# A hybrid attention layer on one core: x given in both layouts, V of all heads made from unnormalised blocks

## The chip, the core and the metric

The kernel runs on one core of a Trainium2 chip. The metric is device time in microseconds (us), the median of three runs. The engines are named as in the profile: PE is TensorE (matmuls; PEld is its weight load), DVE is VectorE, ACT is ScalarE, POOL is GpSimd, and SP's queue issues the DMAs. "Split" below means that a value is kept as two tiles, hi (a copy by ACT, rounded to the matmul's type) and lo (the rest, by DVE), and that a product is then three matmuls: hi by hi, lo by hi, hi by lo.

## What is computed

One layer on x (1024 tokens, D = 1024, float32), followed by a last RMSNorm. What the change touches is the first line and the projections that read it:

```python
h = rmsnorm(x, g_mix)                     # x * rsqrt(mean(x*x, axis=-1) + 1e-6) * g_mix
proj = h @ w_in                           # 1024 x 2560
q, k, v, p, gb, gc, hin = split(proj)     # 512, 512, 512, 256, 256, 256, 256 columns
att  = diff_attention(q1, q2, k1, k2, v)  # 4 heads, causal, two softmaxes, v of 128 columns each
pool = multiscale_pool(p); conv = gb * causal_conv3(gc * hin)
x = x + concat(att, pool, conv) @ w_o
x = x + swiglu(rmsnorm(x, g_ffn)); out = rmsnorm(x, g_final)
```

## The kernel before

**Layout.** PE contracts over partitions, so the projections need h with D on the partitions: h[c] (c is the half of 512 tokens) is a pair of tiles hi and lo of 128 x 8 x 512, element [p, k, t] being feature k*128 + p of token t. x lies in memory with tokens as rows.

**The first stage** (lines 215 to 239) goes token block by token block, 128 at a time. `load` brings x's block (512 KB), `normed` (L129) squares and sums it on ACT (L118), forms the mean on DVE (L103) and the power -1/2 on POOL (L110), and scales with g_mix on DVE (L135). `turn_split` (L139) turns the eight 128 x 128 pieces on PE (L144) into PSUM, and ACT (L145) and DVE (L146) evict them into hi and lo. Between two blocks' transposes stand the 24 matmuls of 128 x 256 (L199) that make V of heads 0 and 1 for an earlier block (`project_v`, L188). V of heads 2 and 3 is made later, as one of the fill items below. Fourteen matmuls on the identity (L93) open PE's queue, ahead of any data.

**The fill.** The other projections are items of `chain` (L390): 128 columns of w_in each, 48 matmuls of 128 x 512 (L248) in 16 steps, the next item's weights split in the middle of the one before. Items are K and Q of head 0 and pool columns 1, which are put ahead of attention (`n_before = 3 * 16`, L410), then K and Q of the other heads, conv and pool columns, and V of heads 2 and 3. Attention's 25 early blocks (head, 128 queries) are worked off in `scores` (L484), `flip`, `attend` and `put`; `pace` (L675) draws the fill's steps between their parts, so that PE has products while DVE and ACT do the softmax. A scheduler then sets the order of each engine's instructions within these dependencies; every engine works its queue in order.

**The bias table.** Lines 430 to 446 make the table of relative biases that every score block adds: a small matmul (L437), an addition on DVE (L439), and three DMAs one after the other (L441, L443, L445), the last into the tile near, which DVE reads at L503.

**Buffers.** 35 slots of 128 x 1024 float32 hold everything passing; PSUM has two buffers each of a (two banks), c and f (one bank).

## Time and profile before

| | |
|---|---|
| median of three runs | 1084.64 us (1084.09 to 1084.82) |
| the profiled execution | 1085.24 us |
| its span, first to last instruction | 1083.3 us |
| PE busy | 1061.3 us (98%) |
| PEld busy | 891.2 us (82%) |
| DVE busy | 745.1 us (69%) |
| ACT busy | 428.1 us (40%) |
| mean granted clock of PE | 0.997 |

A busy share is an average over stages. What a stage's work is worth is read from the chain of waits (what released each step) and from the table of busy time by stage. Matmuls are pipelined: the duration of one is its latency, and the pace is read from a row of them in the chain.

### The profile page before, as it was taken

What the parts mean: (1) busy time and instruction counts of PE and PEld (TensorE: products, weight loads), DVE (VectorE), ACT (ScalarE), POOL (GpSimd) and SP (SyncE); (2) the same over time, 40 slices, a digit from 0 to 9 for tenths busy, and PEclk for the clock granted to TensorE, in tenths of its full rate; (3) what the DMA queues carried; (4) which work ended last, traced back from release to release, by engine and by line L of the source; (5) the groups of instructions that cost most, each with busy time, mean ns of one, the idle gap of its engine ahead of it and who ended that gap; (6) DMA issues with size and microseconds to landing.
All of it is one profiled execution on the core that took longest, in us unless ns stands there. A gap on an engine that the chain in (4) does not pass through costs nothing.

```text
span 1083.3 us, 13855 instructions
## 1 busy us (share of the span) xinstructions
PE 1061.3 (98%) x5215; PEld 891.2 (82%) x5215; DVE 745.1 (69%) x1321; ACT 428.1 (40%) x764; POOL 61.4 (6%) x89
## 2 busy tenths in 40 slices
PE   7999999999999999899999999999999999999997
PEld 7987888997887887778888888888888888888886
DVE  6549668768687646987777776867776757555554
ACT  6325535546463334532232323323232344343442
POOL 1101001001000002200000000000000000000010
PEclk9999999999999999999999999999999999999999
DMA  7310121102251422235535444543544996476553
GB/s 261 98 31 20 40 78 40 40 2 77 88 175 49 147 98 67 87 117 175 185 108 177 174 144 157 194 157 115 175 171 146 315 361 219 138 225 202 177 203 125
DMA packets 96130, 150.60 MB, mean 139 GB/s; under 512 B 7320, under 2 KB 48832, under 8 KB 96064
## 3 DMA queue, kind: packets, MB, share of 16 engines
q1 hardware_dynamic: 96064, 149.72, 41.2%
q8 instruction: 41, 0.67, 0.3%
q14 instruction: 25, 0.20, 0.1%
HBM read 107.49 MB, written 43.00 MB: 139 GB/s over the span
## 4 chain that ended last, share of the span: by engine, by line
PE 84%; DVE 9%; DMA 3%; ACT 2%; issue 1%; POOL 0%; POOLq 0%; SPq 0%; DVEq 0%; ACTq 0%
PE ps_f L904 17%; PE ps_a L904 11%; PE ps_f L248 10%; PE ps_c L904 10%; PE ps_a L1013 9%; PE ps_f L615 6%; PE ps_c L1013 5%; PE ps_f L1013 5%; PE ps_f L199 4%; PE ps_c L539 2%; PE ps_c L526 1%; PE ps_a L496 1%; PE ps_a L495 1%; PE ps_f L261 1%; DVE k_low L291 1%
## 5 line engine op out<-in xcount | busy, mean ns | idle before, releaser
L51 DVE TENSOR_TENSOR lo<-raw,hi 128x1024 fp32r<-128x1024 f32 (+1 forms) x84 | 93.3, 1134 | 78.1 <-ACT hi L50 72.1
L248 PE MATMUL ps_f<-h,w_hi 128*128 128x512 f32 x448 | 140.8, 395 | 0.6 <-ACT pt L384 0.6
L50 ACT CAST hi<-raw 128x1024 fp32r<-128x1024 f32 (+1 forms) x84 | 81.6, 980 | 119.9 <-DMA raw<-in_w_down 28.2
L904 PE MATMUL ps_c<-b,w 128*128 128x512 f32 x528 | 124.4, 390 | 0.0
L904 PEld LDWEIGHTS ps_c<-b,w 128*128 128x128 f32 x528 | 98.8, 188 | 20.3
L248 PEld LDWEIGHTS ps_f<-h,w_hi 128*128 128x128 f32 x448 | 81.6, 188 | 16.6 <-ACT pt L384 0.9
L110 POOL TENSOR_TENSOR rstd<-ms,nhalf 128x1 f32<-128x1 f32 x56 | 35.1, 627 | 935.1 <-DVE ms L103 873.3
L248 PE MATMUL ps_f<-h,w_lo 128*128 128x512 f32 x224 | 87.6, 391 | 0.5 <-DVE w_lo L170 0.5
L51 DVE TENSOR_TENSOR w<-raw,w 128x512 fp32r<-128x512 f32 x66 | 47.5, 720 | 46.0 <-ACT w L50 46.0
L615 PE MATMUL ps_f<-wo_hi,mix 128*128 128x512 f32 x224 | 75.5, 401 | 0.7 <-ACT mix L50 0.7
L50 ACT CAST w_hi<-s 128x1024 fp32r<-128x1024 f32 x44 | 46.0, 1052 | 61.5 <-DVE s L769 54.2
L50 ACT CAST w<-raw 128x512 fp32r<-128x512 f32 x66 | 41.1, 622 | 59.6 <-PE ps_f L904 27.4
L904 PE MATMUL ps_f<-T,w 128*128 128x512 f32 x264 | 63.7, 390 | 0.0
L508 ACT ACTIVATE e<-ps_a,nm 128x128 f32<-128x128 f32 (+7 forms) x64 | 47.2, 744 | 36.5 <-DVE nm L506 29.3
L51 DVE TENSOR_TENSOR w_lo<-s,w_hi 128x1024 fp32r<-128x1024 f32 x44 | 53.6, 1222 | 10.9 <-DMA kept2S<-sum 2.5
L904 PEld LDWEIGHTS ps_f<-T,w 128*128 128x128 f32 x264 | 49.4, 188 | 10.9 <-DVE low L917 0.6
L1013 PE MATMUL ps_a<-lo,hi 128*128 128x512 f32 (+1 forms) x154 | 57.6, 374 | 0.0
L1013 PE MATMUL ps_a<-hi,lo 128*128 128x512 f32 (+1 forms) x154 | 57.6, 374 | 0.0
L1013 PE MATMUL ps_a<-hi 128*128 128x512 f32 (+1 forms) x154 | 57.5, 374 | 0.0
L904 PE MATMUL ps_f<-t,w_hi 128*128 128x512 f32 x176 | 54.5, 389 | 0.0
L904 PE MATMUL ps_f<-b,w_hi 128*128 128x512 f32 x176 | 54.3, 389 | 0.0
L904 PE MATMUL ps_a<-t,w_hi 128*128 128x512 f32 x176 | 54.2, 389 | 0.0
(204 smaller groups left out, 2318.5 us busy)
## 6 DMA issues: line engine op xcount, KB each, us to landing
raw<-in_w_down SPq DMA_DIRECT2D x37, 512.0 KB, 4.5
raw<-in_w_gate SPq DMA_DIRECT2D x22, 512.0 KB, 5.6
raw<-in_w_up SPq DMA_DIRECT2D x22, 512.0 KB, 4.2
raw<-in_w_in SPq DMA_DIRECT2D x20, 512.0 KB, 3.7
raw<-in_x SPq DMA_DIRECT2D x16, 512.0 KB, 4.6
raw<-in_w_o SPq DMA_DIRECT2D x8, 512.0 KB, 4.3
x<-raw SPq DMA_DIRECT2D x8, 512.0 KB, 2.6
x<-x SPq DMA_DIRECT2D x8, 512.0 KB, 7.5
```

What stands on the lines that cost most here:

```text
L50: nc.scalar.copy(hi, src)
L51: lo_eng.tensor_sub(lo, src, hi.bitcast(F32))
L110: nc.gpsimd.tensor_tensor(r, ms, nhalf, op=ALU.pow)
L199: nc.tensor.matmul(ps[:, tt, :], h[t // 4][b][:, k, cols], ws[k // 4][a][:, k % 4, :], start=k == 0 and j == 0, stop=k == KT - 1 and j == 2)
L248: nc.tensor.matmul(ps, w[a][:, k, :], h[c][b][:, k, :], start=k == 0 and j == 0, stop=k == KT - 1 and j == 2)
L261: nc.tensor.matmul(ps, w[a][:, k, :], h[c][b][:, k, :], start=k == 0 and j == 0, stop=k == KT - 1 and j == 2)
L291: nc.vector.tensor_sub(low[own, s, :], ps[own], t[own, s, :].bitcast(F32))
L508: nc.scalar.activation(es[:, :n], ps[:, :n], AF.Exp, bias=nm, scale=1.0, accum_out=z[:, s:s + 1])
L539: nc.tensor.matmul(av[:, :(2 - a) * DV], pts[j // 4][:, a, (j % 4) * P:(j % 4 + 1) * P], rhs, start=j == 0 and a == 0, stop=j == i and a == 1)
L615: nc.tensor.matmul(wo_ps[t][nh], halves[m, t // 4][:, a, cols], wo[m][b][:, nh * 512:(nh + 1) * 512], start=m == SET_A[0] and j == 0, stop ...
L904: nc.tensor.matmul(ps, w[a][:, k, :], h[b][k], start=new and k == 0 and j == 0, stop=k == 3 and j == 2, skip_group_check=not new)
L1013: nc.tensor.matmul(ps, a_op[a][:, j, i * P:(i + 1) * P], b_op[b][:, j, cols], start=start and p == 0, stop=stop and p == 2, skip_group_che ...
```

## The change

The host gives x a second time as x_t, with tokens as columns, so that blocks arrive with D on the partitions and nothing has to be turned. RMSNorm's factor of a token is then a factor of a column of h and of a row of v:

- Blocks of x_t (256 features by 512 tokens) and of V's 512 columns of w_in are loaded in turn. `gained` makes hi and lo of x times g_mix, g_mix being a scalar per partition (the tile gm, loaded as 1024 single elements). `v_products` multiplies this unnormalised h with V's columns of all four heads, 512 wide, as each pair of blocks lands.
- ACT squares the blocks; `square_sum` adds the squares of the eight features of a partition on DVE; `token_rstd` sums over the partitions with matmuls against two columns of ones, and forms the factor of each token, r, as a column of 128 x 4. `v_out` evicts V with r as a scalar. `along` replicates r, turns it with four transposes and copies it into rbc, so that it lies along the tokens.
- K and Q of head 0 for half 0 come from the unnormalised h too, and are multiplied with rbc at eviction (`of_gained`). V of half 1 follows (`second_half`), and behind its products `normalise` overwrites h of either half by the normalised one.
- The first fill item is what is left: K and Q of head 0 for half 1, and pool columns 1. `n_before` is 0; the fill's count of 224 steps is the same. Heads 2 and 3 of V are no item any more.
- V's slots are occupied from the start, so the finished heads 0 and 1 are spilled to memory (`spill`) and read back where the output projection splits them. Two small tiles of the softmax move into one.

```diff
-A_LAG, D_LAG = 3, 2
...
-def turn_split(hn, h, t, ks, ps):
-def transposed(hn, h, t, whole=True):
-def v_load(pair):
-def project_v(pair):
...
+    gm = cst.tile([P, KT], F32, name="gm")
+    nc.sync.dma_start(gm, g_mix.rearrange("(k p) -> p k", p=P))
...
+    for kk in range(KT // 2):
+        x_load(0, kk, kk == 0)
+        wv_raw.append(v_load(kk, kk == 0))
+    kq_raw = [w_load(w_in, K0), w_load(w_in, Q0)]
+    for kk in range(KT // 2):
+        x_load(1, kk, False)
...
+    def v_out(c, tb, ps, scale):
+        t = 4 * c + tb
+        for pair in range(2):
...
+            nc.scalar.activation(o[:, :, 0, :], src, AF.Copy, scale=scale)
+            nc.vector.scalar_tensor_tensor(out=o[:, :, 1, :], in0=src, scalar=scale, in1=o[:, :, 0, :].bitcast(F32),
+                                           op0=ALU.mult, op1=ALU.subtract)
+
+    def gained(c, kk):
+        for k in range(2):
+            n = 2 * kk + k
+            src, (hi, lo) = xt[c, kk][:, k, :], h[c]
+            nc.scalar.activation(hi[:, n, :], src, AF.Copy, scale=gm[:, n:n + 1])
+            nc.vector.scalar_tensor_tensor(out=lo[:, n, :], in0=src, scalar=gm[:, n:n + 1],
+                                           in1=hi[:, n, :].bitcast(F32), op0=ALU.mult, op1=ALU.subtract)
+
+    def v_products(c, n, ps, tbs=range(4)):
+        w = wv[n // 2]
+        for tb in tbs:
+            for j, (a, b) in enumerate(PASSES):
+                nc.tensor.matmul(ps[tb], h[c][b][:, n, tb * P:(tb + 1) * P], w[a][:, n % 2, :],
+                                 start=n == 0 and j == 0, stop=n == KT - 1 and j == 2)
+
+    def square_sum(sqs):
+        for n in (0, 2):
+            nc.vector.tensor_add(sqs[n], sqs[n], sqs[n + 1])
+        nc.vector.tensor_add(sqs[0], sqs[0], sqs[2])
+        total = sqs[1][:, 0, :]
+        nc.vector.tensor_add(total, sqs[0][:, 0, :], sqs[0][:, 1, :])
...
+    def token_rstd(c, both, ps):
+        for tb in range(4):
+            for a in range(2):
+                nc.tensor.matmul(ps[:, 2 * tb:2 * tb + 2], both[:, a, tb * P:(tb + 1) * P], ones,
+                                 start=a == 0, stop=a == 1)
...
+    def along(r, ps):
+        rep = sl.new("rep", (P, 4, P))
+        nc.vector.tensor_copy(rep, r.unsqueeze(2).to_broadcast([P, 4, P]))
+        for tb in range(4):
+            nc.tensor.transpose(ps[:, tb * P:(tb + 1) * P], rep[:, tb, :], ident)
...
+    def normalise(c, rbc):
+        for kk in range(KT // 2):
+            hn = sl.new("hn", PAIR_SHAPE)
+            for k in range(2):
+                nc.vector.scalar_tensor_tensor(out=hn[:, k, :], in0=xt[c, kk][:, k, :],
+                                               scalar=gm[:, 2 * kk + k:2 * kk + k + 1], in1=rbc,
+                                               op0=ALU.mult, op1=ALU.mult)
+            part = slice(2 * kk, 2 * kk + 2)
+            split_exact(nc, h[c][0][:, part, :], h[c][1][:, part, :], hn, nc.vector)
...
+    v_products(0, KT - 2, v_ps)
+    both = square_sum(sqs)
+    kq_ws = [halves_of(raw, W_SHAPE) for raw in kq_raw]
+    v_products(0, KT - 1, v_ps, range(2))
+    stat_ps = bank("a", (P, 2, 512))
+    r0 = token_rstd(0, both, stat_ps[:, 0, :])
+    v_products(0, KT - 1, v_ps, range(2, 4))
+    rbc0 = along(r0, stat_ps[:, 1, :])
+    for tb in (2, 3, 0, 1):
+        v_out(0, tb, v_ps[tb], r0[:, tb:tb + 1])
+    sqs = []
+    for kk in range(KT // 2):
+        gained(1, kk)
+        sqs.append(squares(1, kk))
...
+    def second_half():
+        both = square_sum(sqs)
+        stat = [bank("c") for _ in range(2)]
+        v_ps = [part for t in (bank("a", (P, 2, 512)) for _ in range(2)) for part in (t[:, 0, :], t[:, 1, :])]
+        v_products(1, 0, v_ps)
+        r1 = token_rstd(1, both, stat[0])
+        v_products(1, 1, v_ps)
+        normalise(0, rbc0)
+        rbc1 = along(r1, stat[1])
+        for n in range(2, KT):
+            v_products(1, n, v_ps)
+        normalise(1, rbc1)
+        for tb in range(4):
+            v_out(1, tb, v_ps[tb], r1[:, tb:tb + 1])
...
-    n_before = 3 * 16
+    items = first_columns()
+    n_before = 0
-    items += [(lambda: v_load(1), V_SHAPE, project_v(1), 16, None)]
-    n_fill = 13 * 16 + 32 - 16
+    n_fill = 15 * 16 - 16
...
+        if hd < 2 and i == NT - 1:
+            spill(hd, mixed[hd])
...
+    given["x_t"] = np.ascontiguousarray(given["x"].T)
```

The order of the instructions moves at three places of which the prediction speaks. In these rows a name is a tile (its buffer's number says which); `h_94` and `h_95` are hi and lo of half 0, `h_96` and `h_97` those of half 1.

First, the head of PE's queue. Before:

```order
L93 MATMUL warm<-ident 128x128 x14
L144 MATMUL ps_f<-ident,hn 128x128 x8
L199 MATMUL ps_f<-w_hi,h_94 128x256
L199 MATMUL ps_f<-w_hi,h_95 128x256
L199 MATMUL ps_f<-w_lo,h_94 128x256
```

And now (L228 is `v_products`):

```order
L228 MATMUL ps_f<-wv,h_94 128x512
L228 MATMUL ps_f<-wv,h_95 128x512
L228 MATMUL ps_f<-wv,h_94 128x512 x2
L93 MATMUL warm<-ident 128x128 x14
L228 MATMUL ps_c<-wv,h_94 128x512
L228 MATMUL ps_c<-wv,h_95 128x512
```

The fourteen matmuls on the identity stood first; now four products that need loaded blocks stand ahead of them, and the transposes are gone.

Second, the end of half 0 of V. On DVE, before, a block's statistics stand just ahead of its scaling:

```order
L103 TENSOR_SCALAR ms<-ss 128x1
L435 TENSOR_TENSOR rb<-rb,rb_513 32x4
L170 TENSOR_TENSOR w_lo<-raw,w_hi 128x1024
L207 TENSOR_TENSOR v<-ps_f,v 128x2x128
L135 SCALAR_TENSOR_TENSOR hn<-raw,rstd,gain 128x1024
L146 TENSOR_TENSOR h_95<-ps_a,h_94 128x8x128
```

Now, on DVE (L221 is `gained`, L234 to L237 `square_sum`, L251 the mean in `token_rstd`, L258 the copy in `along`, L212 `v_out`):

```order
L221 SCALAR_TENSOR_TENSOR h_97<-xt,gm,h_96 128x512 x2
L234 TENSOR_TENSOR sq<-sq 128x1024
L557 TENSOR_TENSOR rb<-rb,rb_623 32x4
L584 TENSOR_SCALAR sub_651<-sub_651 128x1
L235 TENSOR_TENSOR sq<-sq 128x1024
L251 TENSOR_SCALAR stat_294<-ps_a 128x4
L237 TENSOR_TENSOR sq<-sq 128x512
L258 COPY rep<-stat_294 128x512
L212 SCALAR_TENSOR_TENSOR v<-ps_f,stat_294,v 128x2x128
```

and on PE at the same place (L260 are the transposes in `along`, L318 is `of_gained`; `ps_a_285` and `ps_a_434` share a buffer of bank a):

```order
L228 MATMUL ps_a_433<-wv_134,h10_96 128x512
L228 MATMUL ps_a_433<-wv_134,h11_97 128x512
L228 MATMUL ps_a_433<-wv_135,h10_96 128x512
L260 MATMUL ps_a_285<-ident_72,rep_303 128x128 x4
L228 MATMUL ps_a_433<-wv_134,h10_96 128x512
L228 MATMUL ps_a_433<-wv_134,h11_97 128x512
L228 MATMUL ps_a_433<-wv_135,h10_96 128x512
L228 MATMUL ps_a_433<-wv_134,h10_96 128x512
L228 MATMUL ps_a_434<-wv_134,h10_96 128x512
L228 MATMUL ps_a_434<-wv_134,h11_97 128x512
L318 MATMUL ps_f_355<-h00_94,w_hi_271 128x512
```

Work on half 1 (gained h, sums of squares) now stands in DVE's queue ahead of half 0's mean, and PE's queue holds the transposes of the replicated factor behind the first three products of half 1, and the first user of the shared buffer eight products in.

Third, the bias table and its first reader. On PE, before, the table's product (L437) stands three products into K of half 0:

```order
L199 MATMUL ps_f<-w_lo,h_96 128x256
L248 MATMUL ps_f<-h_94,w_hi 128x512
L248 MATMUL ps_f<-h_95,w_hi 128x512
L248 MATMUL ps_f<-h_94,w_lo 128x512
L437 MATMUL ps_c<-su,rb 4x384
```

and now (L523 is K of half 1 in the first fill item, L559 the table's product):

```order
L228 MATMUL ps_a<-wv,h_96 128x512
L523 MATMUL ps_f<-h_96,w_hi 128x512
L523 MATMUL ps_f<-h_97,w_hi 128x512
L523 MATMUL ps_f<-h_96,w_lo 128x512
L559 MATMUL ps_c<-su,rb 4x384
```

On DVE the first reader of the table (L626) now stands behind the evictions of K and Q of half 1:

```order
L393 TENSOR_TENSOR k_low<-ps_f,k 64x512
L394 COPY k<-k 64x512
L384 SCALAR_TENSOR_TENSOR q<-ps_f,q 64x512
L626 ISA ps_a,m<-ps_a,near 128x128
L626 ISA m 128x1
```

where before it stood behind pool columns 1:

```order
L282 SCALAR_TENSOR_TENSOR q<-ps_f,q 64x512 x2
L356 COPY win<-pt 128x1
L170 TENSOR_TENSOR w_lo<-raw,w_hi 128x1024
L503 ISA ps_a,m<-ps_a,near 128x128
L503 ISA m 128x1
```

The table's product has moved from the start of the columns to the end of V of all heads, and one column less stands between it and the first score.

## Rows read from the trace of the kernel before

**Rows 1.** The page: busy time of each engine, and the chain's shares by engine.
```profile
PE 1061.3 (98%) x5215; PEld 891.2 (82%) x5215; DVE 745.1 (69%) x1321; ACT 428.1 (40%) x764; POOL 61.4 (6%) x89
...
PE 84%; DVE 9%; DMA 3%; ACT 2%; issue 1%; POOL 0%; POOLq 0%; SPq 0%; DVEq 0%; ACTq 0%
```

**Rows 2.** Busy time by stage: from:to, length, engines' busy us, PE's clock, DMA.
```profile
core 0: us, PE busy (x) PEld busy (x) DVE busy (x) ACT busy (x) POOL busy (x), PEclk, DMA share, GB/s
0.00:10.00 10.00, 6.33 (x38) 5.75 (x38) 2.57 (x5) 4.31 (x6) 1.54 (x9) 1.00 0.79 278
10.00:20.00 10.00, 8.09 (x52) 7.45 (x51) 7.36 (x10) 7.93 (x13) 1.65 (x3) 0.83 1.05 396
...
60.00:70.00 10.00, 10.00 (x46) 8.29 (x45) 3.98 (x5) 3.42 (x5) 0.00 (x0) 1.00 0.18 52
...
80.00:100.00 20.00, 19.27 (x92) 15.51 (x90) 19.27 (x51) 10.20 (x25) 3.50 (x5) 1.00 0.00 1
```

**Rows 3.** Chain of waits, 0 to 120 us: start, length, engine, what.
```profile
0.74 3.72 DMA raw<-in_x
...
5.97 0.56 POOL rstd L110
...
10.96 4.40 PE ps_f L199 x22
...
22.48 2.87 PE ps_f L199 x24
25.35 0.87 PE ps_a L144 x8
...
37.50 5.75 PE ps_f L199 x48
...
44.67 32.21 PE ps_f L248 x141
```

**Rows 4.** Groups by shape, 0 to 150 us: busy us, mean ns of one, idle.
```profile
L118 ACT ACTIVATE hn<-raw 128x1024 f32<-128x1024 f32 x8 | 8.5, 1061 | 2.5 <-DMA raw<-in_x 2.5
L146 DVE TENSOR_TENSOR h<-ps_a,h 128x1024 fp32r<-128x1024 f32 x7 | 8.5, 1219 | 1.1 <-ACT h L145 1.1
L207 DVE TENSOR_TENSOR v<-ps_f,v 128x256 fp32r<-128x256 f32 x8 | 3.3, 418 | 4.5 <-ACT v L206 4.5
L206 ACT CAST v<-ps_f 128x256 fp32r<-128x256 f32 x8 | 3.0, 372 | 9.2 <-PE ps_f L199 6.8 <-DVE v L207 2.4
L135 DVE SCALAR_TENSOR_TENSOR hn<-raw,rstd,gain 128x512 f32<-128x512 f32 x2 | 1.4, 748 | 0.7 <-POOL rstd L110 0.7
L146 DVE TENSOR_TENSOR h<-ps_f,h 128x512 fp32r<-128x512 f32 x2 | 1.4, 689 | 0.8 <-ACT h L145 0.8
L384 ACT ACTIVATE pt<-ps_f,pscale 128x512 f32<-128x512 f32 x2 | 1.4, 688 | 0.4 <-PE ps_f L383 0.3
```

**Rows 5.** DMA issues, 0 to 60 us: KB each, us from issue to landing.
```profile
pscale<-in_pool_scale SPq DMA_DIRECT2D x1, 1.0 KB, 4.2
```

**Rows 6.** Timeline of PE at the start: start, length, instruction.
```profile
1.60 4.80 PE L93 MATMUL warm<-ident 128*128 128x128 f32 x28 [1.60 <-POOL ident masks.py:199]
```

**Rows 7.** Busy time, three stretches of the start (columns as in rows 2).
```profile
8.00:9.00 1.00, 0.69 (x5) 0.42 (x4) 0.26 (x1) 0.88 (x2) 0.00 (x0) 1.00 1.11 428
...
10.00:11.00 1.00, 0.24 (x3) 0.04 (x1) 1.00 (x2) 1.00 (x3) 0.00 (x0) 1.00 1.01 414
...
12.00:13.00 1.00, 1.00 (x7) 1.00 (x6) 0.71 (x3) 1.00 (x4) 0.21 (x1) 0.50 1.02 418
```

**Rows 8.** The bias table: its product in the chain, its DMAs, the last one's landing.
```profile
43.94 0.73 PE ps_c L437 x2
...
45.45 0.28 SPq L441 DMA_DIRECT2D bdram<-su  x1
47.24 0.54 SPq L443 DMA_DIRECT2D brows<-bdram  x1
51.86 0.37 SPq L445 DMA_DIRECT2D near<-brows  x1
...
near<-brows SPq DMA_DIRECT2D x1, 512.0 KB, 3.7
```

More of the change, by code (lines that the diff above doesn't have):

```diff
@@ new lines, in tile_hybrid_block @@
+    wv = [[sl.new("wv", PAIR_SHAPE, F32R) for _ in range(2)] for _ in range(KT // 2)]
+    v_ps = [bank(tag) for tag in "ccff"]
+    sqs = []
+    for kk in range(KT // 2):
+        if kk:
+            gained(0, kk)
+            split_exact(nc, *wv[kk], wv_raw[kk], nc.vector)
+        else:
+            for k in range(2):
+                src, (hi, lo) = xt[0, 0][:, k, :], h[0]
+                nc.scalar.activation(hi[:, k, :], src, AF.Copy, scale=gm[:, k:k + 1])
+                nc.vector.scalar_tensor_tensor(out=lo[:, k, :], in0=src, scalar=gm[:, k:k + 1],
+                                               in1=hi[:, k, :].bitcast(F32), op0=ALU.mult, op1=ALU.subtract)
+                split_exact(nc, wv[0][0][:, k, :], wv[0][1][:, k, :], wv_raw[0][:, k, :], nc.vector)
+        sl.done(wv_raw[kk])
+        sqs.append(squares(0, kk))
+        if kk < KT // 2 - 1:
+            for k in range(2):
+                v_products(0, 2 * kk + k, v_ps)
@@ new lines, in of_gained @@
+    def of_gained(ws, dones):
+        for w, done in zip(ws, dones):
+            ps = bank("f")
+            for k in range(KT):
+                for j, (a, b) in enumerate(PASSES):
+                    nc.tensor.matmul(ps, w[a][:, k, :], h[0][b][:, k, :], start=k == 0 and j == 0,
+                                     stop=k == KT - 1 and j == 2)
+            t = sl.new("scaled", (P, 512))
+            nc.vector.tensor_mul(t, ps, rbc0)
+            done(0, t)
+            sl.done(t)
+    def second_half():
[12 more added lines that the diff above has]
+            v_out(1, tb, v_ps[tb], r1[:, tb:tb + 1])
+        for w in wv:
+            sl.done(*w)
@@ L395, in chain @@
         later = []
-        for n, (_, _, run, middle, then) in enumerate(items):
+        for n, (_, _, run, middle, then, *_) in enumerate(items):
             more = n + 1 < len(items)
```

168 lines of the change are left out of this document (84 added, 84 removed).

## Prediction

> **What bounds the kernel now.** I read the page first: TensorE (PE) is busy 1061.3 of 1083.3 us and makes 84% of the chain that ended last [rows 1]. A change therefore pays what it takes from PE's own work or from its idle time, 22 us in all, and nothing else. The table by stage shows where that idle time lies: 3.67 us of the first 10 us and 1.91 of the next, none from 60 to 70 us, where DVE works 3.98 of 10 us, and 0.73 from 80 to 100 us, where attention begins and DVE is full with 19.27 of 20 [rows 2]. The chain of waits then gives the pace of each kind of work: the first x tile lands at 4.46 us, V products run in rows only from 10.96, V of the first pair ends at 43.25, and the K, Q and pool columns, 141 products in one piece, end at 76.88 [rows 3].
>
> **What PE does less.** A row of 24 V products of 256 columns takes 2.87 us, 0.1196 each; eight transposes take 0.87; a product of 512 columns takes 32.21/141 = 0.2284 [rows 3].
> - Removed: 64 transposes, 8 x 0.87 = 7.0 us.
> - V: 384 x 0.1196 = 45.9 us become 192 x 0.2284 = 43.9: 2.0 less.
> - Added: 8 transposes of the replicated rstd, 0.9, and 16 products of two columns. No row has that shape. Nearest are the 256-column one and the transpose of 128 columns, 0.1196 and 0.109, which hardly differ; I take 0.12, 1.9 in all, and half of it as the lower end, 1 us less.
>
> PE's own work falls by 6.2 us. What it waits for decides the rest, so I follow the stage by the clock.
>
> **The start.** Before, a whole x block has to land, be squared, normalised and turned before V. Now the first V product needs gm, half an x block and half a V block, and one ACT and one DVE piece of 512 on each (0.69 and 0.75 [rows 4]). gm is 1024 single elements and stands first in SP's queue; a load of 256 such elements took 4.2 us [rows 5], the first x tile 3.72 [rows 3]. So gm, issued at about 0.75, lands between 4.5 and 5.5; I take 5, DVE starts at 5.5 and V at 6 to 6.5. The warm-up, which filled PE's idle start (4.80 us for 28 pieces [rows 6]), now stands behind the first four V products: between 28 x 0.109 = 3.1 and 4.8 us. I cost it at nothing, because PE's next wait covers it; without that cover it is the 3.1 to 4.8 us.
>
> **The wait for rstd of half 0** is the term that decides. For PE, V of half 0 is 96 x 0.2284 = 21.9 us, the warm-up up to 4.8, the sums' products 1.0, and the slow clock as before: 10 to 20 us had a mean of 0.83, thus 1.7 us lost [rows 2, 7]. From 6.3 it is through at 34.0 to 35.7. Then come three V products of half 1 and the transposes of the replicated rstd, and that is late. DVE's queue holds ahead of it, by [rows 4], 16 pieces of gained h at 0.75 (12.0), the V splits 2 x 0.69 + 3 x 1.22 (5.0), two K and Q splits (2.4), six additions of squares of 1024 (7.3), one of 512 and a low half (1.4) and small ones (0.5): 28.6 us from 5.5. ACT needs 2 x 0.69 + 2 x 1.06 = 3.5 us per pair of blocks where DVE needs 2.7, and holds DVE up by some 1.5 us while the first blocks pass. So the mean is formed at 35.6, the power takes 0.56 [rows 3] and two hops, the copy 0.69: PE goes on at 37.2, having idled 1 to 3 us. Three of the six additions are of half 1, which nobody needs yet.
> Next, bank a: the eighth V product of half 1 needs the statistics' bank back. ACT frees it after five V evictions (0.37 [rows 4], with a scale of its own 0.1 more) and a copy, at 39.3; PE is there at 38.3: 1.0 us.
>
> **To the end of Q.** From 37.2: 93 V products 21.2, 96 of K and Q 21.9, transposes 0.9, two-column products 1.0, the bias table's product 0.7 [rows 8], the bank 1.0: 83.9 us. V ends at 72.3. DVE has 34 us of work meanwhile: 16 x 0.75 and 8 x 1.22 for normalising h in place, 10 V evictions at 0.42, eight pieces of K and Q at 0.69, 2.7 of others. Its last piece of h waits for V's end and takes 1.06 + 1.22: 74.6. PE wants it 18 products after V, at 76.4. So normalising is hidden, with 2 us to spare; every us that DVE loses beyond that is one of PE.
>
> **The sum.** Before, pool 1 ends at 76.9 and V of the second pair, 192 x 0.1196 = 23.0, is still to come among attention: 99.9. After, Q ends at 83.9 and pool 1, 48 x 0.2284 = 11.0, is still to come: 94.9. That is 5.0 us less. The filling steps of attention stay 224. DVE is rid of eight V evictions and two splits there, 5.8 us; PE idles 0.73 in its worst 20 us [rows 2], so I give nothing for it. Spilling two heads and reading them back adds transfers that have a hundred us to land: nothing, at most 0.5.
>
> **Start of attention.** The bias table comes late now. Its product stands three products into half 1 of K, at 73; its addition on DVE is done at about 74. Before, from there to the landed table it took from 45.45 to 51.86 + 3.7 = 55.6 us, three transfers one behind the other [rows 8], so now it lands at 84.2. Its first reader stands in DVE's queue behind Q's eviction (85), so the table itself costs little; but K's split for the next head and all scores, exps and flips start only there, while PE has 15 pool products, 3.4 us, before it needs a bank from them. Between 0 and 3.4 us of waiting I take 1, nearest to the 0.73 of the stage that is alike [rows 2].
>
> **The total.** Profiled execution 1085.24 - 5.0 + 1.0 = 1081.2. The median of the runs lies 0.60 below that execution: 1080.6.
>
> **Rivals.**
> - *The clock falls a second time.* From 8 to 11 us PE was busy 0.69 to 0.24 of the time, and behind that the granted clock was 0.50, the 1.2 GHz level [rows 7], at a cost of 1.7 us [rows 2]. The wait for rstd could do it again: 1082.3. Against it, PE is full for 28 us ahead of this wait, which it was not at the start. [...] Chance 0.13, 0.03 of it within 0.2%.
> - *DVE is not late at 35 us*: the wait for rstd and the bank's 1.0 vanish, 1076.6 to 1078. Chance 0.12.
> - *The feed is slower*: gm or the blocks land later, or ACT holds DVE up at every piece. DVE has no slack ahead of 35 us, so each us counts in full; 2 to 5 us give 1082.6 to 1085.6. Chance 0.15.
> - *The bias table makes it slower.* Each us by which DVE's addition is late delays table, scores and exps, and PE waits with its queue in order once the 3.4 us of pool products are used. From 8 us late the gain is gone, at 11 it is 1084.6 + 3 = 1087.6. That takes DVE's 34 us of work a third over its rows, with ACT at the same banks. Against it, rows of one shape differ by little. Chance 0.10.
> - *V is no cheaper at 512 columns*: 2 us less, 1082.6; K's products of this shape speak against it. It lies at the edge of the forecast.
>
> **Chances.** The forecast, 1078 to 1082.4, has 0.50. A measurement of this kernel tells 0.2%, 2.2 us, from no change. Faster: 0.50 + 0.12 + 0.10 = 0.72. Same: 0.15 + 0.03 = 0.18. Slower: 0.10. The range, 1076 to 1085, takes in all but the slower rival and the end of the slow feed.
>
> **What would show it.** Right: V products from 6 to 6.5 us; PE idle just ahead of the transposes of the replicated rstd, ended at about 37 us by DVE's copy; Q done at 83 to 85; the table landed at 84 to 85; behind it the same rows as before, some 4 us early. Wrong: no wait at 34 to 37 us; a second stretch at 0.50; PE idle by more than 3.4 us between 84 and 95; a gap between V and K of half 1 at 72 to 76 us, which would mean that DVE is late with h.

## The result and the profile after

The changed kernel took 1090.13 us (median of 6 runs, 1088.15 to 1093.94) against 1084.37 of the kernel before on the same chip: ratio 1.0057, 95% interval 1.0037 to 1.0077. It is slower by 5.8 us; the forecast was 1080.6, and its range ended at 1085. One execution of 1351.72 us, at a mean granted clock of 0.731, is left out of the medians below.

The page of the changed kernel, the line that answers to [rows 1]:

```profile
PE 1057.0 (97%) x4983; PEld 876.2 (80%) x4983; DVE 768.3 (71%) x1353; ACT 440.2 (40%) x776; POOL 58.7 (5%) x84
```

The span is 1089.3 us. PE's work fell by 4.3 us, where 6.2 were forecast, and its idle time rose from 22.0 to 32.3. The table by stage says where. First the changed kernel, columns as in [rows 2]:

```profile
0.00:10.00 10.00, 2.98 (x10) 2.55 (x11) 3.20 (x6) 5.66 (x8) 0.80 (x8) 1.00 0.79 252
...
70.00:80.00 10.00, 7.21 (x31) 4.93 (x30) 5.31 (x13) 4.16 (x11) 0.72 (x1) 1.00 0.05 12
...
80.00:315.00 235.00, 228.71 (x1193) 191.60 (x1192) 179.48 (x473) 122.00 (x295) 24.41 (x38) 1.00 0.20 63
315.00:441.00 126.00, 121.81 (x617) 100.61 (x616) 81.05 (x191) 49.47 (x125) 13.77 (x18) 0.99 0.33 107
```

Then the kernel before, the stages that [rows 2] leave out:

```profile
70.00:80.00 10.00, 10.00 (x48) 8.35 (x47) 4.22 (x10) 2.65 (x5) 0.00 (x0) 1.00 0.00 1
80.00:315.00 235.00, 232.48 (x1308) 201.08 (x1307) 179.00 (x470) 122.02 (x295) 22.95 (x36) 1.00 0.17 54
315.00:441.00 126.00, 123.21 (x637) 101.94 (x637) 82.35 (x195) 54.47 (x132) 15.44 (x20) 1.00 0.32 109
```

PE's idle time, before and after: 5.58 and 7.02 us up to 20 us (the changed kernel's all in the first 10), none and 2.79 from 70 to 80, 2.52 and 6.29 from 80 to 315 (attention and its fill), 2.79 and 4.19 from 315 to 441 (output projection). Behind 441 the two run alike: the first product behind the output projection stands at 435.05 and 440.66 us, the last one of the kernel at 1076.74 and 1082.02.

Four places on PE show where time is lost, each in the one profiled execution of its kernel, which lies up to 2.5 us beside the median (the edited kernels come below). The last filling product, in the kernel before and in the changed one:

```profile
315.50 0.39 PE L261 MATMUL ps_f<-h,w_lo 128*128 128x512 f32 x1
```

```profile
318.35 0.39 PE L363 MATMUL ps_f<-h,w_lo 128*128 128x512 f32 x1
```

| us | K of half 0 starts | Q of half 1 is done | last filling product starts | last product of the output projection starts |
|---|---|---|---|---|
| kernel before | | | 315.50 | 434.83 |
| changed kernel | 38.76 | 86.4 | 318.35 | 440.43 |
| setup early | 41.13 | 87.5 | 318.77 | 437.04 |
| bias table alone early | 39.96 | 87.6 | 318.78 | 438.25 |
| V moved, in the kernel before | | | 319.38 | 437.37 |
| pace alone | 38.11 | 82.6 | 313.57 | 433.95 |
| best run | 34.52 | 79.7 | 311.75 | 434.12 |

The wait at 75 us, in the timeline of PE and then of DVE (start, length, instruction, in brackets the idle time before it and who ended it):

```profile
75.22 0.61 PE L523 MATMUL ps_f<-h,w_hi 128*128 128x512 f32 x2
78.62 0.30 PE L618 MATMUL ps_a<-k,q 128*128 128x128 f32 x1 [2.79 <-DVE v L212]
```

```profile
68.03 1.22 DVE L50 TENSOR_TENSOR h<-hn,h 128x1024 fp32r<-128x1024 f32 x1
73.46 0.29 DVE L575 TENSOR_TENSOR su<-su 128x128 f32<-128x128 f32 x1 [4.21 <-DMA su<-in_lambda_k]
73.67 0.48 DVE L212 SCALAR_TENSOR_TENSOR v<-ps_a,stat,v 128x256 fp32r<-128x256 f32 x1
```

L618 is the first score product of attention. It stands in PE's queue 17 products into K of half 1, and it wants a buffer of bank a. Both buffers are held by V of half 1 until DVE evicts it (L212), and DVE's queue has a product of the lambda vectors (L575) ahead of that, whose loads land at 73.3. The chain of waits of the same kernel shows these loads and, behind them, the bias table:

```profile
67.49 5.84 DMA su<-in_lambda_k
...
78.11 1.33 DMA bdram<-su
...
79.46 4.66 DMA brows<-bdram
...
84.14 4.25 DMA near<-brows
...
88.41 0.30 DVE ps_a L626
```

The table lands at 88.4, not at the forecast's 84.2. In the kernel before SP issued the lambda loads at 19 to 21 us; now they stand behind the first stage, and SP issues them at 66 to 68 us.

### The profile page after: what moved, and what is told of

Its sections match the earlier page's. It is cut to its first block, busy times and chain, and to the rows that moved or that the text cites. A ratio compares the mean times of both kernels' runs of the same rounds, so it can differ in the third digit from the quotient of the medians.

```text
span 1089.3 us, 13436 instructions
## 1 busy us (share of the span) xinstructions
PE 1057.0 (97%) x4983; PEld 876.2 (80%) x4983; DVE 768.3 (71%) x1353; ACT 440.2 (40%) x776; POOL 58.7 (5%) x84
## 4 chain that ended last, share of the span: by engine, by line
PE 80%; DVE 8%; DMA 4%; ACT 3%; issue 1%; POOL 0%; SPq 0%; POOLq 0%; DVEq 0%; ACTq 0%
PE ps_f L1029 17%; PE ps_a L1029 11%; PE ps_c L1029 10%; PE ps_a L1138 9%; PE ps_f L350 8%; PE ps_f L738 6%; PE ps_c L1138 5%; PE ps_f L1138 5%; PE ps_f L363 2%; PE ps_c L660 2%; PE ps_a L618 1%; PE ps_a L619 1%; PE ps_c L647 1%; PE ps_f L318 1%; ACT e L631 1%
## 5 line engine op out<-in xcount | busy, mean ns | idle before, releaser
L50 DVE TENSOR_TENSOR lo<-raw,hi 128x1024 fp32r<-128x1024 f32 (+1 forms) x84 | 93.2, 1132 | 77.1 <-ACT hi L49 71.5
L350 PE MATMUL ps_f<-h,w_hi 128*128 128x512 f32 x384 | 122.1, 397 | 0.0
L350 PEld LDWEIGHTS ps_f<-h,w_hi 128*128 128x128 f32 x384 | 69.9, 189 | 12.9 <-ACT pt L486 0.3
L50 DVE TENSOR_TENSOR w<-raw,w 128x512 fp32r<-128x512 f32 x66 | 46.5, 705 | 46.2 <-ACT w L49 46.0
L110 POOL TENSOR_TENSOR rstd<-ms,nhalf 128x1 f32<-128x1 f32 x48 | 29.0, 605 | 900.6 <-DVE ms L103 841.2
L350 PE MATMUL ps_f<-h,w_lo 128*128 128x512 f32 x192 | 75.1, 391 | 0.0
L50 DVE TENSOR_TENSOR w_lo<-s,w_hi 128x1024 fp32r<-128x1024 f32 x44 | 53.4, 1218 | 10.2 <-DMA kept8S<-sum 2.3
```

The source lines that it names most:

```text
L50: lo_eng.tensor_sub(lo, src, hi.bitcast(F32))
L110: nc.gpsimd.tensor_tensor(r, ms, nhalf, op=ALU.pow)
L350: nc.tensor.matmul(ps, w[a][:, k, :], h[c][b][:, k, :], start=k == 0 and j == 0, stop=k == KT - 1 and j == 2)
```

## The experiments

Theories. **1**: the late setup (lambdas, bias table) is the loss. **2**: attention itself got slower, because V of heads 2 and 3 no longer fills it. **3**: spilling two heads costs the output projection. **4** and **5**: the start is lost to PE's order, or to DVE's load. Each ratio is to the kernel before on the same chip, from five rounds.

### Setup early, and the table alone early

```diff
+    rb = cst.tile([32, HEADS], F32, name="rb")
...
+    sl.done(su, su2, su3)
+
     wv = [[sl.new("wv", PAIR_SHAPE, F32R) for _ in range(2)] for _ in range(KT // 2)]
...
     fill_to(1)
-    rb = cst.tile([32, HEADS], F32, name="rb")
...
-    sl.done(su, su2, su3)
```

> The changed kernel with its whole small-setup block (bias table, lambdas, pool weights) written ahead of the V weights' tiles, so that its slots and its places in the queues come early, as in the kernel before. Theory 1 (the late setup is the loss): the 2.8 us in which TensorE stands at 75.8 to 78.6 us behind the lambda loads go, and the first reader of the bias table (88.4 us now) runs at about 83 to 85; with what the late start costs behind it some 5 us come back: 1084 to 1086 us, ratio to the kernel before 1.000 +- 0.002. Rival 2 (attention itself is slower, because all 224 filling steps are spread over it, and two heads are spilled): only the 2.8 us come back at most, 1087 to 1088, and the blocks from 150 to 290 us keep their 2 to 3 us of lag.

> The changed kernel with the bias table alone moved early (a slot of its own); lambdas and pool weights stay late. Theory 1a (the late table is the part that costs): the first reader of the table comes at about 85 instead of 88.4 us, and 2 to 3 us come back: 1087 to 1088. Theory 1b (it is the vector engine's 4.2 us wait for the lambda loads that costs): that wait stays, the time stays within 1 us of the changed kernel's 1090.1, and only the setup moved as a whole gains. Rival 2: no change either, and none from the whole block.

The whole setup early: 1087.37 us, ratio 1.0021 (1.0011 to 1.0032). The table alone: 1087.93, 1.0028 (1.0019 to 1.0037). By stage, setup early:

```profile
70.00:80.00 10.00, 10.00 (x46) 8.11 (x45) 7.44 (x14) 4.31 (x10) 0.00 (x0) 1.00 0.16 48
80.00:315.00 235.00, 228.90 (x1190) 192.42 (x1189) 179.49 (x471) 122.14 (x295) 23.98 (x38) 0.99 0.18 58
```

By the ratios 3.9 and 3.1 us come back, the same by the intervals. They do not come back where theory 1 has them. With the whole setup early the 2.79 us at 75 are gone and the table's first reader runs at 79.06 instead of 88.41, but K of half 0 starts 2.4 us later (41.13; the bias table's product, 0.7 us, and waits of 0.59 and 0.48 stand ahead of it), so that Q of half 1 is done at 87.5, later than in the changed kernel, and the last filling product starts at 318.77 against 318.35. From 80 to 315 us PE idles 6.10 us against 6.29. With the table alone early PE still waits 2.04 us between 70 and 80, and the time is that of theory 1a all the same, not of 1b. But the earlier first reader (79.09) does not give it: Q of half 1 is done at 87.6.

What the profiled executions gain, they gain in the output projection. There PE waits for a tile that is written to memory behind the last fill and read back. The chain of waits of the changed kernel, then with the setup early:

```profile
319.49 4.53 DMA mix<-y
...
324.03 4.86 DMA raw<-mix
```

```profile
319.92 3.27 DMA mix<-y
...
323.21 4.09 DMA raw<-mix
```

In the changed kernel PE idles 2.13 us for it, at 327, and has a granted clock of 0.50 from 330 to 332, the 1.2 GHz level; with the setup early neither is there. The kernel before has the same two transfers (4.69 and 3.73 us) and idles 0.71. Why they took longer in the one execution is open. So these two runs do not show what the wait at 75 costs; the run with the pace alone, below, does.

### The spill alone, in the kernel before

```diff
+        if hd < 2 and i == NT - 1:
+            spill(hd, mixed[hd])
...
-            if m >= HEADS:
+            if m != 2:
```

> The kernel before with one part of the change alone: heads 0 and 1 are spilled to DRAM after their last block and read back for the output projection. Theory 3 (spilling costs the output projection): the last filling product to the first of the output projection and from there to its end takes 2 to 3 us longer, as in the changed kernel (119.3 to 122.1 us from the last filling product to the last of the output projection), total 1086 to 1087.5, and the product that waits for the tile read back shows a wait of some 2 us. Rival: the transfers are hidden, within 0.5 us of the kernel before (1084.4 to 1084.9), and the loss there belongs to something else.

1084.65 us, ratio 0.9999 (0.9990 to 1.0007): no cost. Theory 3 falls. The 2.8 us that the stage from the last filling product to the end of the output projection grew by in the changed kernel (119.3 to 122.1) is not the spill: with the spill alone that stage takes 118.1 us, with the setup early 118.3.

### V of heads 2 and 3 ahead of attention, in the kernel before

```diff
     items = qk_columns(0) + pool_columns(1)
-    n_before = 3 * 16
+    items[2:2] = [(lambda: v_load(1), V_SHAPE, project_v(1), 16, None)]
+    n_before = 4 * 16
...
-    items += [(lambda: v_load(1), V_SHAPE, project_v(1), 16, None)]
...
-    n_fill = 13 * 16 + 32 - 16
+    n_fill = 14 * 16 - 16
```

> The kernel before with V of heads 2 and 3 moved from the middle of attention to ahead of it (behind Q of head 0; heads 0 and 1 spilled, so that the slots suffice): the same 208 filling steps stand in attention as in the changed kernel, its first stage stays the old one. No operation is added. Theory 2 (attention loses because 23 us of V products no longer fill it, while the vector engine has what it had): TensorE's lost time from 80 to 315 us rises from some 6 to 9 to 11 us, total 1087.5 to 1089.5. Rival (the loss in attention comes from the new first stage: late table, slots, lag of the vector engine): within 0.7 us of the kernel before.

1087.78 us, ratio 1.0025 (1.0014 to 1.0036), with the spill that costs nothing and no other operation more. Two things move: V's 32 steps go ahead of attention, and with 64 steps counted as done there, the 16 of pool columns 1 come into it, as in the change. This is theory 2: the exchange costs 2.7 us (1.5 to 3.9) with the old first stage. Which of the two costs it, V gone or pool columns 1 in, was not separated. DVE is busy 118.7 us between 100 and 250, against 111.0 before: V's 32 steps gave PE 23.0 us and DVE only 5.8, and pool columns 1 bring window sums. Most of the time goes at one place; by stretches of 2 us:

```profile
266.00:268.00 2.00, 0.00 (x0) 0.00 (x0) 1.97 (x4) 1.39 (x4) 0.00 (x0) 1.00 0.20 59
268.00:270.00 2.00, 1.99 (x6) 1.60 (x7) 2.00 (x11) 1.50 (x4) 0.55 (x1) 0.56 0.00 0
270.00:272.00 2.00, 2.00 (x7) 1.56 (x6) 1.97 (x5) 1.50 (x5) 0.00 (x0) 0.58 0.00 0
```

PE stands still (2.05 us in one piece), and behind that works at half clock for some 3.5 us, 1.7 us lost. The same wait is in the runs with the even pace and 208 steps below, 2.05 to 2.06 us. In the kernel before, V's 32 steps stand between pool columns 0 and K and Q of head 3 (V's products from 203 to 235 us), and at Q of head 3 DVE has one long piece ahead of the short one (L544) behind which PE's flip waits; PE idles 0.56 us:

```profile
260.79 1.23 DVE L170 TENSOR_TENSOR w_lo<-raw,w_hi 128x1024 fp32r<-128x1024 f32 x1 [0.38 <-ACT w_hi L167]
262.05 0.35 DVE L544 SCALAR_TENSOR_TENSOR att<-ps_c,r,att 128x128 f32<-128x128 f32 x1
```

Without V between them a window sum of pool columns 0 (L369, 1.22 us) joins that piece, as the lines under "Which bursts" show for the run with the pace alone.

### The pace of the fill

```diff
-    n_before = 0
+    n_before = 16
...
-    n_fill = 15 * 16 - 16
+    n_fill = 14 * 16 - 16
```

First on top of the early setup, then as the only edit of the changed kernel:

> The changed kernel with the setup early, and K and Q of half 1 counted as done ahead of attention (16 steps before, 208 shared over all 25 blocks), so that the first two blocks get filling steps as well and the later ones 8% fewer each. Theory 2c (the steps stand in the wrong blocks: none in the first two, where the vector engine is busy with the pool's windows): the waits at 116 to 147 us shrink by 1 us or more, 1086 to 1086.5. Rival 2b (too few steps in all): what the first blocks gain the later ones lose, 1087 to 1088.

> The changed kernel with one number changed: K and Q of half 1 counted as done ahead of attention (16 steps before, 208 shared over all 25 blocks); the setup stays late. If late setup and uneven pace are two causes that add: the 2.8 us at 75 stay, some 2.7 us come back behind it, ratio to the kernel before about 1.003, 1087 to 1088. Rival (the pace only helps once the setup is early, since the late table holds the first blocks anyway): under 1 us, 1089 to 1090.

With the setup early 1084.72 us, 1.0002 (0.9992 to 1.0012). Alone: **1083.62 us, 0.9996 (0.9988 to 1.0005)**; these two numbers take back all that the change lost, and by the ratios 6.6 us. One premise of the first expectation was mistaken: the first blocks did have filling steps, namely K and Q of half 1 themselves. What the edit does is put those 16 steps ahead of the first score product, and give each block 8.3 steps on average instead of 9.0. In the run with the pace alone the lambda loads are about as late as ever, and the table is 1.7 us earlier (chain of waits):

```profile
66.81 5.47 DMA su<-in_lambda_k
...
83.10 3.63 DMA near<-brows
...
86.87 0.12 DVE ps_a L626
```

but PE idles only 0.27 us from 70 to 80, and that for h (L50). By stage, and the first score product in the timeline, now behind Q of half 1:

```profile
70.00:80.00 10.00, 9.73 (x41) 6.95 (x40) 5.92 (x15) 4.82 (x11) 0.73 (x1) 1.00 0.08 18
80.00:315.00 235.00, 230.74 (x1201) 194.64 (x1201) 183.23 (x477) 122.88 (x295) 24.01 (x38) 0.99 0.22 69
```

```profile
82.33 0.39 PE L523 MATMUL ps_f<-h,w_lo 128*128 128x512 f32 x1
82.56 0.22 PE L618 MATMUL ps_a<-k,q 128*128 128x128 f32 x1
```

The wait at 75 needs the late loads and the score product in front of Q, and goes with either. Here its end is seen: Q of half 1 is done 3.8 us earlier than in the changed kernel, 0.65 of it from an earlier start of K. The two causes do not add as forecast (1087 to 1088).

> Early setup and even pace, with all 224 steps shared over the 25 early blocks instead of 208 (none left for the last blocks). Theory 2b (attention lacks filling steps): the waits at 122 and 261 us (1.8 and 2.2 us) shrink by 1 us or more in all; what the last seven blocks lose without steps stands against it: 1083 to 1086 in all. Rival 2a (the waits come from bursts of long pieces on the vector engine): the waits move and keep their size, and the end without steps makes it 1 us or more slower than the even pace alone.

```diff
-    n_fill = 14 * 16 - 16
+    n_fill = 14 * 16
```

All 224 steps in the early blocks, on top of setup early and even pace: 1087.64 us, 1.0032 (1.0020 to 1.0043). PE idles 5.64 us from 80 to 300, and 3.13 from 300 to 341 where the last blocks have no steps left; the run with setup early and even pace has 3.86 and 0.74. More steps per block do not help; a step brings DVE work with its products. Theory 2b, as a mere lack of steps, falls.

### Which bursts

> The changed kernel with the setup early, and the two pool columns exchanged: pool 0 (two windows on the vector engine) stands first, pool 1 (four windows) 96 steps later. Theory 2a (the burst of window sums, now inside the first blocks, makes the vector engine late for the evictions that TensorE waits for): the 1.8 us lost at 116 to 118 and some of the 1.5 at 147 go, and 1 to 2 us come back: 1085.5 to 1086.5, unless the same burst costs as much later. Rival 2b (any arrangement with 208 steps loses the same): the waits move to other places, 1087 to 1088.

```diff
-        cols = qk_columns(0) + pool_columns(1)
+        cols = qk_columns(0) + pool_columns(0)
```

and pool columns 1 in the later place: 1086.41 us, 1.0019 (1.0010 to 1.0028), the same as without by the intervals. From 100 to 120 us PE's idle time fell from 1.46 us to none, and from 240 to 260, where pool columns 1 now stand, it rose from none to 0.91: the waits follow the window sums, as 2a has it, and no gain is left. What such a wait is made of, from the run with the pace alone, DVE, ACT and PE:

```profile
258.29 1.23 DVE L147 TENSOR_TENSOR w_lo<-raw,w_hi 128x1024 fp32r<-128x1024 f32 x1
259.53 1.22 DVE L471 SCALAR_TENSOR_TENSOR mean<-win,pt 64x1024 f32<-64x1024 f32 x1
260.79 0.35 DVE L665 SCALAR_TENSOR_TENSOR att<-ps_c,z,att 128x128 f32<-128x128 f32 x1
```

```profile
260.79 1.04 ACT L49 CAST ph<-mean 128x1024 fp32r<-128x1024 f32 x1 [2.12 <-DVE mean L471]
261.74 0.27 ACT L118 ACTIVATE ps_c<-att 128x128 f32<-128x128 f32 x1
```

```profile
262.19 0.33 PE L647 MATMUL ps_c<-ident,e 128*128 128x128 f32 x1 [2.06 <-ACT ps_c L118]
```

Two long pieces on DVE, then one on ACT, stand ahead of two short ones (0.35 and 0.27 us) that free bank c, and PE's queue holds the flip that wants it.

### The first stage

> The changed kernel with the warm-up products kept ahead of the first V product on TensorE, and one tiny ScalarE copy of a constant ahead of everything, so that the load of ScalarE's function table no longer stands behind the wait for the first x block. Theory 4 (the start costs): the 3.4 us of warm-up behind the first V products leave TensorE's path and 1.3 us of table load leave ScalarE's; the vector engine is next by 0.7 to 2 us, so V of half 0 and everything behind it come 1.5 to 2 us earlier: 1088 to 1088.6. Rival (the lead is lost at the next wait, the vector engine's work to the end of V): the rows behind 75 us stand where they stood, 1090 +- 0.5.

```diff
+    nc.scalar.copy(cst.tile([P, 4], F32, name="table"), nhalf4)
...
-                v_products(0, 2 * kk + k, v_ps)
+                with tc.issue_after(warmed.ins):
+                    v_products(0, 2 * kk + k, v_ps)
```

1091.46 us, 1.0055 (1.0040 to 1.0070), no gain on the change's 1.0057. PE is through V of half 0 at 30.9 us instead of 35.5, and waits for the replicated rstd; timeline, and the clock behind it:

```profile
35.48 0.66 PE L261 MATMUL ps_a<-ident,rep 128*128 128x128 f32 x4 [4.56 <-DVE rep L259]
```

```profile
36.00:40.00 4.00, 4.00 (x13) 3.15 (x12) 4.00 (x10) 3.02 (x8) 0.00 (x0) 0.57 0.01 2
```

So DVE sets the pace here, and the warm-up behind the first products was covered, as forecast, but for 0.7 us, by which the transposes come earlier than the changed kernel's. That lead is lost: the half clock behind the wait costs 1.7 us, and K of half 0 starts at 40.3, not 38.8.

> The changed kernel with the setup early, ScalarE's function table loaded early, the warm-up first on TensorE, and the transposes of the replicated rstd of half 0 moved behind the first 12 products of K. Theory 4b (the start is lost to the wait for rstd, 4.7 us when the warm-up comes first): K of half 0 starts some 3 us earlier than with the setup early alone, and 1 to 2 us of it reach the end of Q: 1085.5 to 1086.5. Rival (the vector engine's whole work to the end of V sets the end of this stage, whatever TensorE does before): Q ends where it ended, 1087 to 1088.

```diff
-    rbc0 = along(r0, stat_ps[:, 1, :])
...
+                if k == 4 and not turned:
+                    with tc.issue_after(last.ins):
+                        turned[0] = along(r0, stat_ps[:, 1, :])
```

1091.75 us, 1.0062 (1.0048 to 1.0075), inconclusive on its question: the bias table's product, early in PE's queue, waited 4.83 us at 22 us for a 32 x 4 subtraction that is late on DVE.

> The changed kernel with the setup early, the even pace, and at the start: the warm-up first on TensorE, ScalarE's function table loaded early, the bias table's product held behind the sums' products, the transposes of the replicated rstd behind 12 products of K. Theory 4b (TensorE's start is what is lost): K of half 0 starts 1 to 2 us earlier than with the even pace alone, and 1 us or more of it reaches the end: 1083 to 1083.7. Rival 5 (the vector engine sets the end of the stage): TensorE waits longer at the sums' products instead, the time stays, 1084 to 1085.4.

```diff
-    nc.tensor.matmul(bps[:HEADS, :384], rb, oh, start=True, stop=True)
+    with tc.issue_after(ones_end[0].ins):
+        nc.tensor.matmul(bps[:HEADS, :384], rb, oh, start=True, stop=True)
```

With that product held back, and the even pace: 1087.74, 1.0032 (1.0020 to 1.0045). PE waited 5.66 us from 31.5, until DVE had formed the mean (34.37), copied the rstd and added the bias table (36.60), whose product holds a buffer of bank a; it had a mean clock of 0.83 from 30 to 50, and K of half 0 starts at 41.6, not earlier than 40.4. Rival 5 holds for this run.

> The changed kernel with the setup early and the even pace (16 steps counted ahead of attention), and the additions of the squares (one of half 0, all of half 1) moved from the vector engine to GpSimd: 6.1 us of 1.22 us pieces less on the vector engine up to 60 us. Theory 5 (the vector engine's work, not TensorE's, sets the end of the first stage): K of half 0 starts 1 to 3 us earlier, Q of half 1 ends 2 to 3 us earlier, total 1082 to 1083. Rival (what the vector engine saves is lost again at the next wait, or GpSimd slows it at their common port): within 0.7 us of the even pace alone, 1084 to 1085.4.

> The run with the additions of the squares on GpSimd, and the window sums of the pool columns there as well: some 8 us of pieces of 1.1 us leave the vector engine in the first blocks, 4 us later. Theory 2a (bursts of long pieces on the vector engine keep it from the evictions TensorE waits for): the waits at 122 to 124 us shrink by 1 us or more and the total falls by 1 to 2 us against the run before this one. Rival (the powers of the rstd's on GpSimd come late behind the sums, or the common port slows the vector engine): no gain, or up to 2 us more.

> All of it together: setup early, even pace, sums of squares and windows on GpSimd, and the start as in the run before this one. If TensorE's start and the vector engine's load limit the first stage in turn (4b and 5 together), the two gains add, 1080 to 1082; if one of them alone sets it, the time is that of the better single run.

```diff
-            nc.vector.tensor_add(sqs[n], sqs[n], sqs[n + 1])
+            (nc.gpsimd if n == 0 else eng).tensor_add(sqs[n], sqs[n], sqs[n + 1])
...
-                nc.vector.tensor_add(w2[rows, length:], src[rows, length:], src[rows, :-length])
+                nc.gpsimd.tensor_add(w2[rows, length:], src[rows, length:], src[rows, :-length])
```

Squares' additions on GpSimd 1091.87 (1.0070, 1.0057 to 1.0082), window sums too 1094.75 (1.0100, 1.0085 to 1.0116), all with the start 1095.51 (1.0104, 1.0091 to 1.0118). All are slower than the even pace (1.0002), and theory 5 was not tested by them, since DVE lost more than it was spared: K of half 0 starts at 45.2 in the first of them, not at 40.4. Timeline of the first of them, POOL, then DVE:

```profile
31.51 3.16 POOL L234 TENSOR_TENSOR sq<-sq 128x1024 f32<-128x1024 f32 x1 [1.35 <-ACT sq L200]
34.74 2.37 POOL L235 TENSOR_TENSOR sq<-sq 128x1024 f32<-128x1024 f32 x1
```

```profile
32.34 2.47 DVE L305 TENSOR_TENSOR su<-su 128x128 f32<-128x128 f32 x1
34.74 2.93 DVE L221 SCALAR_TENSOR_TENSOR h<-xt,gm,h 128x512 fp32r<-128x512 f32 x1
```

In the even pace, without GpSimd at work, the same two lines take 0.27 and 0.73 us. Here they end at 34.81 and 37.67, GpSimd's additions at 34.67 and 37.11.

> Early setup and even pace, with the additions of half 1's squares held on the vector engine behind the replicated rstd of half 0 (nothing added or removed). Theory 5 (the vector engine's work ahead of the rstd of half 0 sets TensorE's resumption): the mean of half 0 waited 1.36 us for TensorE in the even pace, so the lead of 2.4 us on the vector engine shows only as a longer wait there and K of half 0 starts within 0.5 us of 40.4; total within 0.7 us of the even pace. If K starts earlier by 1 us or more, the vector engine was the limit there after all.

> The run with the additions held, and the warm-up first on TensorE, the bias table's product behind the sums' products. Now TensorE is through V of half 0 at about 30 and the vector engine is lighter by 3.6 us of additions and 0.9 of setup ahead of the mean: it is formed at 31 to 32.5, K of half 0 starts at 36.5 to 38, and 1 to 3 us of that reach the end of Q: 1082 to 1084. Rival (the vector engine has the same work up to V's end): the additions make the normalising of h late instead, Q of half 1 ends where it did (84.4), and the time stays at 1084 to 1085.4.

```diff
-        both = square_sum(sqs)
+        with tc.issue_after(rep_ins[0].ins):
+            both = square_sum(sqs)
```

Order alone: the additions of half 1's squares behind the replicated rstd of half 0 give 1084.00, 0.9998 (0.9989 to 1.0007), the same as the even pace. K of half 0 starts at 39.35, though, 1.09 us earlier, so by the sign set down for it DVE was the limit there. With the warm-up first as well, and the bias table's product behind the sums' products, **1081.78, 0.9974 (0.9964 to 0.9985)**: now DVE is through with half 0 when PE comes, K of half 0 starts at 36.2 and Q of half 1 ends at 80.9. In total time DVE's order gave nothing alone, nor did PE's in the runs above that had it; added to DVE's, PE's gave 2.6 us (0.9998 to 0.9974).

> The changed kernel, setup late as it has it, with three edits of order: 16 steps ahead of attention and 208 shared, the additions of half 1's squares held behind the replicated rstd of half 0, the warm-up first on TensorE. If the early setup is of no use by itself, this is as fast as the best run: ratio to the kernel before 0.996 to 0.998, 1080 to 1082, Q of half 1 done at 79 to 81 us. Rival (the late lambda loads hold the vector engine in front of V's evictions, which matters again when TensorE comes earlier): TensorE waits 1 to 3 us at 68 to 72 us ahead of K of half 1, and the time is that of the run with the pace alone, 1083.6.

The best, with the setup left late: **1081.42, 0.9969 (0.9956 to 0.9981)**, 3.4 us faster than the kernel before, and by the ratios 9.5 faster than the change. Timeline of DVE and of PE at the rstd of half 0:

```profile
29.98 0.14 DVE L251 TENSOR_SCALAR stat<-ps_a 128x4 f32<-128x4 f32 x1
31.33 0.43 DVE L260 COPY rep<-stat 128x512 f32<-128x512 f32 x1 [1.21 <-POOL stat L252]
```

```profile
31.82 0.66 PE L262 MATMUL ps_a<-ident,rep 128*128 128x128 f32 x4 [1.35 <-DVE rep L260]
```

Q of half 1 ends at 79.7, and PE waits 0.75 us at 72 for h (L50), where the rival had 1 to 3. The edits are the pace, the two edits of order, and nothing else: the early setup is of no use by itself.

## Why the prediction was wrong

**The sum, term by term.** The prediction had 5.0 us less up to the columns, 1.0 more at the start of attention, and nothing behind: 4.0 less. In the profiled execution the first stage gave 5.3 without its wait at 75, the start of attention cost 2.8, attention with its fill 5.4 (to the last filling product), and the output projection 2.8: 5.6 more at its end.

**The first stage was worth what was forecast, and more once nothing stood in it.** V started at 7.0, not 6 to 6.5: gm landed 2.2 us after its issue, earlier than thought, but ACT loads its function table only behind the wait for x:

```profile
4.18 1.28 ACT L288 ACT_TABLE_LOAD   x1 [4.18 <-DMA xt<-in_x_t]
5.48 0.72 ACT L288 ACTIVATE h<-xt,gm 128x512 fp32r<-128x512 f32 x1
```

The mean of half 0 was formed at 34.1 (35.6 forecast), where DVE had waited 0.71 us for PE; the power took 1.33 us (0.56 taken from [rows 3], where it is 128 x 1). PE went on at 36.2 (37.2 forecast) without a wait, lost 0.40 at the bank (1.0 forecast), and K of half 0 started at 38.8. Q of half 1 ended at 86.4 against 83.9; without the 2.79 us at 75 that is 83.6, and 82.6 in the run with the pace alone. Add pool 1's 11.0 us and compare with 99.9: 2.5 us gained in the changed kernel, 6.3 with the pace alone, 9.2 in the best run; 5.0 was the forecast. Little of it reaches the end: 0.4 us (not told from none by its interval) and 3.4 against the kernel before.

**The step that failed most is "The filling steps of attention stay 224 ... so I give nothing for it."** The count stayed; what the steps are did not. V's 23.0 us of PE work with little DVE work left, and pool columns 1 came in with much; the prediction counted the 5.8 us that DVE is rid of, and not that PE is rid of 23.0 that stood between DVE's long pieces. PE's idle time from 80 to 315 went from 2.52 to 6.29 us, and attention with its fill took 5.4 us longer. The exchange alone, in the kernel before, makes it 3.7 longer by the same count, and the whole time 2.7. The even pace did not heal this: with it alone the stage is still 4.4 us longer, in the best run 5.4, and both have the wait of 2.05 us at 258 to 262 with a half clock behind it; in the run of 1081.78 us, where the clock stayed up behind that wait, it is 2.3. How the rest divides between fewer steps per block and their place was not separated.

**The other failed step is the start of attention.** The prediction took 1 us there, between 0 and 3.4, "nearest to the 0.73 of the stage that is alike". The stage is not alike: the rows of order ahead of the prediction show DVE's first reader of the table behind Q, but on PE the first score product stands in the middle of K of half 1, only 14 products behind the table's own. The bound of 3.4 was the time that pool products cover PE, but PE works its queue in order and met a score product in front of them. What held it was bank a, through DVE's queue, and in that queue loads that the prediction had not timed: it followed the bias table, not the lambdas. PE idled 2.79 us.

**Nothing was given for the output projection** either. It took 2.8 us more in the profiled execution, with the wait of 2.13 us at 327 and the half clock behind it. From the last filling product to its end this stage takes 118.0 us to 122.4 in the runs whose edits do not touch it, so it is open whether the change has a part in those 2.8.

**The small terms** held: the spill is free, normalising h keeps PE waiting 0.27 us in the run with the pace alone, eight two-column products took 0.95 us. PE's own work fell by 4.3 us instead of 6.2; which term was short was not followed up. **The rivals**: "the bias table makes it slower" had the right sign, at 0.10, and the wrong price: a table landing at 86.7 instead of the forecast's 84.2 costs nothing when PE has other products, as the run with the pace alone shows. "DVE is not late at 35 us" is what happened in the changed kernel: the profile shows no wait of PE at the transposes, which the prediction had as a sign of being wrong, and DVE waited for PE. The time given for it did not come, because the loss lies behind. "The clock falls a second time" at the rstd did not happen there, but in two runs that brought PE there earlier: behind waits of 4.56 and 5.66 us the granted clock was 0.50 to 0.64, behind the 1.35 us of the best run it stayed at 1.00.

## What to carry to other kernels

When work moves from a filler to an earlier stage, count what the remaining filler asks of the other engines per step, and which long pieces of theirs the filler had kept apart. Look, too, where in the queue the first instruction stands that needs a buffer held by a late eviction: PE had other products behind the score product, and still stood 2.79 us in front of it. Set the pacing numbers anew after such a move; here two numbers were worth 6.6 us. Two engines that limit a stage in turn may show no gain from either edit alone, so try the pair. And when an edit removes a wait and the time falls by about as much, follow the later milestones before calling that wait the cause: with the setup early 2.79 us of wait went and the medians fell by 2.8, and yet the profiled execution had gained nothing up to the last filling product.

## What the hardware showed that was not expected

GpSimd's additions held DVE up. On DVE a 128 x 128 multiplication took 2.47 us and a 128 x 512 piece of gained h 2.93, both with two inputs in SBUF, beside additions of 128 x 1024 on GpSimd; without these they took 0.27 and 0.73. The Trainium skill, "SBUF — State Buffer", section "SBUF: two separate sides", says that the two engines' common port pair is locked for a whole instruction, for a VectorE one with two SBUF inputs only against a GpSimd one that reads SBUF, so that the other blocks; the trace agrees, as each piece ends 0.1 to 0.6 us behind GpSimd's addition.

PE's clock does not fall after every wait of one length. It read 1.00 up to 84 us behind the 2.79 us at 75.8 in the changed kernel, but behind 2.06 us from 260.1 in the run with the pace alone it went from the 2.4 to the 1.2 GHz level:

```profile
262.00:264.00 2.00, 1.81 (x7) 1.44 (x8) 2.00 (x10) 1.51 (x5) 0.55 (x1) 0.75 0.00 0
264.00:266.00 2.00, 2.00 (x6) 1.61 (x5) 1.97 (x6) 1.66 (x5) 0.00 (x0) 0.50 0.00 0
266.00:268.00 2.00, 2.00 (x9) 1.62 (x8) 1.94 (x3) 0.59 (x1) 0.00 (x0) 0.90 0.00 0
```

That is 1.7 us on top of the wait (0.25, 0.50 and 0.10 of 2 us each), nearly its own size again. In the run of 1081.78 us the same wait, 2.06 us at 257.9, left the clock at 1.00.

The power of 128 x 4 elements on GpSimd took 1.33 us in the changed kernel, where that of 128 x 1 took 0.56 in the kernel before. The load of ACT's function table, 1.28 us, stood behind the wait for x, at 4.18 us, in the changed kernel; in the kernel before, and with a tiny copy ahead of it, it ran at 0.73. Why it waited in the one and not in the others is open.
